# Two of eight row-tile pairs of an up-projection in seven block products

## The chip, the core and the metric

The kernel runs on one core of a Trainium2 chip. The metric is the device time of one execution in microseconds (us). The median of three runs of the kernel before is 1767.04 us (1766.61 to 1767.25).

The engines that matter here are TensorE (PE in the profile; PEld is its weight load), VectorE (DVE), ScalarE (ACT), GpSimd (POOL), which issues some transfers, and SyncE (SP), which issues the weight loads. Each engine takes its instructions strictly in the order in which the built program has them.

## The reference

One decoder layer on 256 tokens of width 2048, all in fp32. An input projection of 16896 columns feeds a gated linear recurrence (16 heads) and a dilated attention (12 heads). Their outputs are projected, gated, added and projected once more (`w_out`) onto the residual. Then comes the part that the change touches, the convolutional feed-forward, and a last RMSNorm:

```
hup = u @ w_up                       # (256, 2048) @ (2048, 11264)
hc  = causal depthwise conv of width 3 over the tokens of hup, + conv_b
a, b = hc[..., :5632], hc[..., 5632:]
h   = h + (gelu(a) * b) @ w_down     # (256, 5632) @ (5632, 2048)
```

## The kernel before

**Three matmuls per product.** An fp32 operand is split into two float32r parts: `hi`, the operand rounded to float32r by a copy on ACT, and `lo`, the rest `raw - hi`, computed on DVE. Each product of an activation block and a weight block is the sum of three float32r matmuls: low activation by `hi` weight, high by `hi`, high by `lo` (lines 386, 387 and 388 of `moving_step`). The activations are the stationary operand (128x128), the weights the moving one (128x512).

**The weight stream.** All weights lie in memory in the order of their use, cut into units of sixteen 128x128 tiles (1 MB each). `stream_spec` writes that order down. `load` fetches a unit into one of three `raw` buffers on SP's queue. `split` makes `hi` and `lo` of it in two halves of 128x1024 (lines 248 and 249), each in a pool of four buffers. `next_tiles` splits two units ahead and loads three ahead of the unit in use.

**The feed-forward.** `w_up` is worked through in 11 blocks of 512 columns of the first half (`ua0` to `ua10`) and 512 of the second (`ub0` to `ub10`). For each, `moving` accumulates 16 row tiles and two token halves into two of four main PSUM banks (`psm`). `up` then scales the banks on ACT, transposes them on PE into side banks (`pss`, four), and runs the convolution on ACT and DVE (lines 800 to 802). After the gate and another split (`ff`), `w_down` follows in two parts (`PARTS`): after six blocks and after the other five, each adding to the residual `h`.

**What sets the order.** Apart from the first stage, the order of each engine's instructions is made by a scheduler at build time from the order of the code, the buffers and the dependencies. It puts instructions of other work between those that would have to wait.

Of the kernel before, what the change touches and what calls it, by code (L numbers as in the profile page):

```python
# [33 lines left out]
PARTS = ((0, 6), (6, NBLK))  # L34
EPS = 1e-6
UNIT = 16
LOOKAHEAD = 2
# [108 lines left out]
def hybrid_block(ctx, tc, x_p, x_t, weights, g1, gf, params, c_rope, c_mask0, c_mask1, c_level, out):  # L148
# [39 lines left out]
    raws, splits = {}, {}  # L188
# [34 lines left out]
    xu = [w4([2, 2, T], f"xu{i}", F32R) for i in range(KD // 2)]  # L223
# [8 lines left out]

    def split(u):
        if u >= NUNITS or u in splits:
            return
        load(u)
        parts = []
        half = UNIT * P // 2
        for s in range(2):
            hi = wp.tile([P, half], F32R, tag="hi", name=f"hi{u}_{s}", bufs=4)  # L240
            lo = wp.tile([P, half], F32R, tag="lo", name=f"lo{u}_{s}", bufs=4)
            n = 2 if u == 0 else 1
            w = half // n
            for q in range(n):
                raw = raws[u][:, s * half + q * w : s * half + (q + 1) * w]
                if u < KD // 2 and q == 0:
                    split_x(2 * u + s)
                last[0] = act.activation(hi[:, q * w : (q + 1) * w], raw, AF.Copy)  # L248
                last[1] = vec.tensor_tensor(lo[:, q * w : (q + 1) * w], raw, hi[:, q * w : (q + 1) * w].bitcast(F32), op=ALU.subtract)  # L249
            parts.append((hi, lo))  # L250
        splits[u] = parts
# [29 lines left out]

    def next_tiles(n):

        i = pos[0]
        u, r = divmod(i, UNIT)
        if r == 0:
            for v in range(u, u + LOOKAHEAD + 1):
                split(v)
            load(u + LOOKAHEAD + 1)
            pump(SIDE_US)  # L290
# [99 lines left out]
    def moving(parts, k0, nk, name):  # L390

        pst = [main_bank(f"{name}_{m}") for m in range(2)]
        for k in range(k0, k0 + nk):
            moving_step(pst, parts, k, k0, nk)
        return pst

# [146 lines left out]
    def hgrn_side(g, f, k, q, gt, v):  # L543
# [22 lines left out]
        for li, b in enumerate(LEVELS):  # L566
            ps = side_bank(f"lv{g}_{b}")
            psv = ps.rearrange("p (m h t) -> p m h t", m=2, h=HG)
            ks = sb.tile([P, M], F32, tag="o2", name=f"ks{g}_{b}", bufs=6)
# [22 lines left out]
            if b < 64:  # L592
                new = sb.tile([P, half], F32, tag=f"tot{b}", name=f"tot{g}_{b}", bufs=1)
# [8 lines left out]
        a01 = sb.tile([P, HG, P], F32, tag="a01", name=f"a01_{g}", bufs=1)  # L602
# [4 lines left out]
        for m in range(2):  # L607
# [6 lines left out]
            sq = sb.tile([P, M], F32, tag="o2", name=f"osq{g}_{m}", bufs=6)  # L614
# [7 lines left out]
            o1 = sb.tile([P, HG, P], F32, tag="o2", name=f"oo{g}_{m}", bufs=6)  # L622
# [70 lines left out]
    drain()  # L693

# [9 lines left out]
    mixed = [[w4([4, 2, P], f"mix{j}_{m}", F32R) for m in range(2)] for j in range(NJ)]  # L704
# [4 lines left out]

    def stage(name):  # L710
        return sb.tile([P, 512], F32, tag="o2", name=name, bufs=6)
# [29 lines left out]
    hv = [w4([2, 2, T], f"hv{i}", F32R) for i in range(KD // 2)]  # L741

    def hv_parts(k, m):
        t = hv[k // 2][:, k % 2]
        return t[:, 0, m * P : (m + 1) * P], t[:, 1, m * P : (m + 1) * P]
# [16 lines left out]
    for j in range(NJ):  # L762
# [4 lines left out]
        for i in range(2):  # L767
            pt = side_bank(f"ht{j}_{i}").rearrange("p (c t) -> p c t", c=2)
            for c in range(2):
                for m in range(2):  # L770
                    n = (2 * i + c) * P
                    pe.transpose(pt[:, c, m * P : (m + 1) * P], h[:, m, n : n + P], ident)
            for c in range(2):
                k = 4 * j + 2 * i + c
                d = hv[k // 2][:, k % 2]
                act.activation(d[:, 0], pt[:, c], AF.Copy, scale=pc("g2", k))
                vec.scalar_tensor_tensor(d[:, 1], pt[:, c], pc("g2", k), d[:, 0].bitcast(F32), op0=ALU.mult, op1=ALU.subtract)
# [3 lines left out]


    def up(b, c0, name):

        pst = moving(hv_parts, 0, KD, name)
        ups = []
        for m in range(2):
            u = stage(f"{name}u{m}")
            act.activation(u, pst[m], AF.Copy, scale=rstd2[:, m : m + 1])
            ups.append(u)  # L790
        t = w4([FB, T], f"{name}c")
# [14 lines left out]
    for part, (b0, b1) in enumerate(PARTS):  # L806
        ff = [w4([2, 2, T], f"ff{part}_{i}", F32R) for i in range((b1 - b0) * FB // 2)]
        for b in range(b0, b1):
            a = up(b, b * FB, f"ua{b}")
# [5 lines left out]
            g = up(b, NFF + b * FB, f"ub{b}")  # L815
# [6 lines left out]
        if part:  # L822
# [72 lines left out]
```

## Time and profile before

| | |
|---|---|
| median of the runs shown | 1767.04 us |
| the profiled execution's own time | 1768.19 us |
| its span, first to last instruction | 1766.4 us |
| mean granted TensorE clock | 0.998 |
| PE busy | 1749.9 us (99% of the span) |
| DVE busy | 1092.5 us (62%) |
| ACT busy | 888.6 us (50%) |
| memory read | 321.41 MB, 183 GB/s over the span |
| instructions | 21297 |

A row of groups gives line, engine, operation, the tile written and those read, shapes and count; then total busy time and the mean of one in ns; then the engine's idle time just ahead of them, with what ended it. A matmul's mean (390 ns) is from its start to its modelled end; since matmuls overlap, the distance from one start to the next is what a matmul costs. A row of the timeline gives start and duration in us; "x2" merges neighbours. The up-projections of the first six blocks run from about 1024 to 1298 us, `w_down`'s first part to 1427 us, the other five blocks to 1655 us, its second part to 1754 us.

### The profile page before, as it was taken

Reading aid. Unit: us, or ns where it says so; the run is one execution under the profiler, and the core shown is the slowest. Engines: PE = TensorE matmul, PEld = TensorE weight load, DVE = VectorE, ACT = ScalarE, POOL = GpSimd, SP = SyncE. Lnnn points to the kernel's source line nnn. Section 1 sums busy time; section 2 is a strip of 40 time slices with the busy share of each in tenths; the row PEclk is TensorE's granted clock in tenths of the full one; section 3 lists DMA queues with packets and bytes.
Section 4 is the critical chain, followed back from the end, with each engine's and each line's share of the span. In section 5 each row is a group of like instructions: output and inputs, shape, how many; then the busy total and the mean of one; then the engine's idle time right before and its main releaser. Section 6 shows DMA issues by size and latency. Waiting matters only on the chain.

```text
span 1766.4 us, 21297 instructions
## 1 busy us (share of the span) xinstructions
PE 1749.9 (99%) x8472; PEld 1463.5 (83%) x8472; DVE 1092.5 (62%) x1295; ACT 888.6 (50%) x1084; POOL 9.4 (1%) x24
## 2 busy tenths in 40 slices
PE   9999999999999999999999999999999999999997
PEld 7888888888888888888888888888888888888885
DVE  7765575777768675445565556666664456666654
ACT  6444465545454555444445455555543345555442
POOL 0000000000000000000000000000000000000000
PEclk9999999999999999999999999999999999999999
DMA  7665634544444444555556555455555554555552
GB/s 274 220 209 201 228 143 145 179 165 179 167 167 167 166 168 167 191 190 191 191 185 227 185 191 185 177 186 191 182 189 196 196 188 176 184 215 185 188 197 98
DMA packets 48371, 328.02 MB, mean 186 GB/s; under 512 B 5600, under 2 KB 5856, under 8 KB 10128
## 3 DMA queue, kind: packets, MB, share of 16 engines
q1 hardware_dynamic: 45648, 318.28, 50.7%
q0 software_dynamic: 1472, 5.24, 1.1%
q10 hardware_dynamic: 1152, 3.15, 0.5%
q8 instruction: 66, 1.08, 0.2%
q14 instruction: 33, 0.27, 0.0%
HBM read 321.41 MB, written 2.10 MB: 183 GB/s over the span
## 4 chain that ended last, share of the span: by engine, by line
PE 97%; DVE 1%; DMA 1%; ACT 0%; issue 0%; SPq 0%; DVEq 0%; ACTq 0%
PE ub L387 5%; PE ub L386 5%; PE ub L388 5%; PE ua L387 5%; PE ua L388 5%; PE ua L386 5%; PE dn L387 5%; PE dn L386 5%; PE dn L388 5%; PE egp L388 3%; PE egp L386 3%; PE egp L387 3%; PE ak L299 3%; PE aq L299 2%; PE wo L388 2%; PE gp L387 2%
## 5 line engine op out<-in xcount | busy, mean ns | idle before, releaser
L249 DVE TENSOR_TENSOR lo<-raw,hi 128x1024 fp32r<-128x1024 f32 (+1 forms) x602 | 734.5, 1221 | 575.5 <-ACT hi L248 565.9
L248 ACT ACTIVATE hi<-raw 128x1024 fp32r<-128x1024 f32 (+1 forms) x602 | 636.0, 1057 | 763.3 <-PE dn L387 127.3
L387 PE MATMUL ub<-hi,hv 128*128 128x512 f32 x352 | 139.2, 395 | 0.0
L387 PE MATMUL ua<-hi,hv 128*128 128x512 f32 x352 | 138.8, 394 | 0.0
L387 PE MATMUL dn<-hi,ff 128*128 128x512 f32 x352 | 137.4, 390 | 0.0
L386 PE MATMUL ub<-hi,hv 128*128 128x512 f32 x352 | 137.3, 390 | 0.0
L386 PE MATMUL ua<-hi,hv 128*128 128x512 f32 x352 | 137.3, 390 | 0.0
L388 PE MATMUL ub<-lo,hv 128*128 128x512 f32 x352 | 137.2, 390 | 0.0
L388 PE MATMUL ua<-lo,hv 128*128 128x512 f32 x352 | 137.2, 390 | 0.0
L386 PE MATMUL dn<-hi,ff 128*128 128x512 f32 x352 | 137.1, 390 | 0.0
L388 PE MATMUL dn<-lo,ff 128*128 128x512 f32 x352 | 137.1, 389 | 0.0
L386 PE MATMUL egp<-hi,xu 128*128 128x512 f32 x256 | 100.7, 393 | 0.0
L388 PE MATMUL egp<-lo,xu 128*128 128x512 f32 x256 | 99.9, 390 | 0.0
L387 PE MATMUL egp<-hi,xu 128*128 128x512 f32 x256 | 99.8, 390 | 0.0
L386 PEld LDWEIGHTS ub<-hi,hv 128*128 128x128 f32 x352 | 66.1, 188 | 14.0
L386 PEld LDWEIGHTS dn<-hi,ff 128*128 128x128 f32 x352 | 66.1, 188 | 13.8
L386 PEld LDWEIGHTS ua<-hi,hv 128*128 128x128 f32 x352 | 66.1, 188 | 13.8
L388 PEld LDWEIGHTS dn<-lo,ff 128*128 128x128 f32 x352 | 66.1, 188 | 13.6
L387 PEld LDWEIGHTS dn<-hi,ff 128*128 128x128 f32 x352 | 66.1, 188 | 13.5
L388 PEld LDWEIGHTS ua<-lo,hv 128*128 128x128 f32 x352 | 66.2, 188 | 13.1
L387 PEld LDWEIGHTS ua<-hi,hv 128*128 128x128 f32 x352 | 66.2, 188 | 13.0
L388 PEld LDWEIGHTS ub<-lo,hv 128*128 128x128 f32 x352 | 66.2, 188 | 13.0
(435 smaller groups left out, 3154.9 us busy)
## 6 DMA issues: line engine op xcount, KB each, us to landing
raw<-weights SPq DMA_DIRECT2D x298, 1024.0 KB, 4.8
h<-x_t ACTq DMA_DIRECT2D x4, 512.0 KB, 7.5
xt<-x_p SPq DMA_DIRECT2D x3, 512.0 KB, 10.3
xs_q<-aqraw POOLq DMA_DIRECT2D x6, 256.0 KB, 6.8
xs_k<-akraw POOLq DMA_DIRECT2D x6, 256.0 KB, 7.2
raw<-weights SPq DMA_DIRECT2D x4, 256.0 KB, 4.8
raw<-weights SPq DMA_DIRECT2D x2, 512.0 KB, 8.1
gfb<-gf POOLq DMA_DIRECT2D x2, 512.0 KB, 6.6
```

The source lines that it names most:

```text
L248: last[0] = act.activation(hi[:, q * w : (q + 1) * w], raw, AF.Copy)
L249: last[1] = vec.tensor_tensor(lo[:, q * w : (q + 1) * w], raw, hi[:, q * w : (q + 1) * w].bitcast(F32), op=ALU.subtract)
L299: pe.matmul(ps, hi, pair, start=(k == 0), stop=False, skip_group_check=True)
L386: pe.matmul(pst[m], xl, hi, start=(k == k0), stop=False)
L387: pe.matmul(pst[m], xh, hi, start=False, stop=False)
L388: pe.matmul(pst[m], xh, lo, start=False, stop=(k == k0 + nk - 1))
```

## The change

The 16 row tiles of a `w_up` block are taken as eight pairs, and a pair's product with the two column halves is a product of two 2x2 block matrices: token halves by row tiles, and row tiles by column blocks. The string `UP_PAIRS = "SPAPSAPA"` gives each pair one of three modes.

- **S** (two pairs): Strassen's method, in the form with seven products and shared sums. `split_s` forms four sums of weight blocks (`q1` to `q4`) on DVE and splits seven blocks into `hi` and `lo` rather than four; 21 matmuls.
- **P** (three pairs): eight products, 24 matmuls, arranged so that they add into the same seven PSUM banks. The activation differences `d1` and `d2` are operands.
- **A** (three pairs): as P, but the `lo` part of the unit's second half is made by ACT writing `-hi` (a copy of raw rounded, scaled by -1) and a transfer from POOL that adds `raw` to it in SBUF.

`sevenfold` accumulates a whole block in seven banks: four main ones and three side ones. `unfold` reads them back: four ACT copies and seven DVE instructions give the four 128x512 results (`c11`, `c21` for the first column half, `c12`, `c22` for the second), which `convolved` transposes as before. `operands` makes the sums of activation blocks once per pair, after the last `w_out` product. `w_down` is done in four parts rather than two, and the SBUF pools are rearranged: some close when their stage ends, and the S splits have a pool of their own. In the first block the pairs are taken in the order 1, 2, 0, 3, 5, 4, 6, 7.

The diff, cut to its core:

```diff
-PARTS = ((0, 6), (6, NBLK))
+PARTS = ((0, 3), (3, 6), (6, 9), (9, NBLK))
+UP_PAIRS = "SPAPSAPA"
+STAGES = 8
...
+    def split_s(u):
+        r = raws[u].rearrange("p (b n) -> p b n", b=4)
...
+        q = pool.tile([P, 2, 512], F32, tag="q", name=f"q{u}", bufs=1)
+        ah, al = pair_tiles(wp, (("hi", 4), ("lo", 4)), "sa")
+        eh, el = pair_tiles(pool, (("se", 4), ("se", 4)), "se")
+        fh, fl = pair_tiles(pool, (("se", 4), ("se", 4)), "sf")
+        g = pool.tile([P, 2, 512], F32R, tag="sg", name=f"sg{u}", bufs=1)
+        vec.tensor_tensor(q[:, 0], r[:, 0], r[:, 3], op=ALU.add)
+        two_parts(ah, al, r[:, 0:2])
+        vec.tensor_tensor(r[:, 3], r[:, 3], r[:, 2], op=ALU.add)
+        vec.tensor_tensor(q[:, 1], q[:, 0], r[:, 2], op=ALU.add)
+        two_parts(eh, el, r[:, 2:4])
+        vec.tensor_tensor(r[:, 0], q[:, 1], r[:, 1], op=ALU.add)
+        two_parts(fh, fl, q[:])
+        two_parts(g[:, 0], g[:, 1], r[:, 0])
...
                 last[0] = act.activation(hi[:, q * w : (q + 1) * w], raw, AF.Copy)
-                last[1] = vec.tensor_tensor(lo[...], raw, hi[...].bitcast(F32), op=ALU.subtract)
+                if s and MODES.get(u) == "A":
+                    act.activation(lo, raw, AF.Copy, scale=-1.0)
+                    nc.gpsimd.dma_start(lo, raw, accum_op=ALU.add)
+                else:
+                    last[1] = vec.tensor_tensor(lo[...], raw, hi[...].bitcast(F32), op=ALU.subtract)
...
+    PRODUCTS = {
+        "S": ((1, "a11", "11"), (7, "x3", "q3"), (6, "x2", "q2"), (2, "a12", "21"), (4, "a22", "q4"), (5, "x1", "q1"), (3, "x4", "22")),
+        "P": (
+            (2, "a11", "11"), (2, "a12", "21"), (4, "a21", "11"), (4, "a22", "21"),
+            (5, "a21", "12"), (5, "a22", "22"), (3, "d1", "12"), (3, "d2", "22"),
+        ),
+    }
+    PRODUCTS["A"] = PRODUCTS["P"]
...
+    def sevenfold(ops, modes_of, order, name):
+        banks = {i: (main_bank if i < 5 else side_bank)(f"{name}_{i}") for i in range(1, 8)}
...
+        for i in order:
+            w = next_pair()
+            for b, x, n in PRODUCTS[modes_of[i]]:
+                (xh, xl), (wh, wl) = ops[i][x], w[n]
...
+                pe.matmul(banks[b], xl, wh, start=b in fresh, stop=False)
+                pe.matmul(banks[b], xh, wh, start=False, stop=False)
+                pe.matmul(banks[b], xh, wl, start=False, stop=left[b] == 0)
...
+    def unfold(p, r, name):
...
+        act.activation(t, p[1], AF.Copy)
+        vec.tensor_tensor(v, p[6], t, op=ALU.subtract)
+        c11, c21, c12, c22 = (stage(f"{name}c{n}") for n in ("11", "21", "12", "22"))
+        act.activation(c11, p[1], AF.Copy, scale=r0)
+        act.activation(c12, v, AF.Copy, scale=r0)
+        act.activation(c21, v, AF.Copy, scale=r1)
+        vec.scalar_tensor_tensor(c21, p[7], r1, c21, op0=ALU.mult, op1=ALU.add)
+        vec.scalar_tensor_tensor(c11, p[2], r0, c11, op0=ALU.mult, op1=ALU.add)
+        vec.scalar_tensor_tensor(c22, p[5], r1, c21, op0=ALU.mult, op1=ALU.add)
+        vec.scalar_tensor_tensor(c12, p[5], r0, c12, op0=ALU.mult, op1=ALU.add)
+        vec.scalar_tensor_tensor(c21, p[4], r1, c21, op0=ALU.mult, op1=ALU.subtract)
+        vec.scalar_tensor_tensor(c12, p[3], r0, c12, op0=ALU.mult, op1=ALU.add)
...
-            a = up(b, b * FB, f"ua{b}")
+            a0, a1, g0, g1_ = unfold(sevenfold(hv, UP_PAIRS, up_order(b), f"up{b}"), rstd2, f"up{b}")
+            a = convolved((a0, a1), b * FB, f"ua{b}")
...
-            g = up(b, NFF + b * FB, f"ub{b}")
+            g = convolved((g0, g1_), NFF + b * FB, f"ub{b}")
```

How the change moves instructions is shown at three places; with the change, all three are where block 1 ends and block 2 begins. In the rows a number after a tile's name is the unit of the weight stream (`lo184`) or the block (`up1c11`); the last number is the buffer's own. Unit 184 is the S pair with which block 2 begins, 185 a P pair, and 181 is the A pair in sixth place of block 1.

First, VectorE where a block's sums are finished. Before (here the first half of block 2, `ua2`), only the splits of the next units and the convolution stand there:

```order
L249 TENSOR_TENSOR lo187_1_8699<-raw187_8668,hi187_1_8698 128x1024
L249 TENSOR_TENSOR lo188_0_8729<-raw188_8702,hi188_0_8728 128x1024
L249 TENSOR_TENSOR lo188_1_8733<-raw188_8702,hi188_1_8732 128x1024
L249 TENSOR_TENSOR lo189_0_8763<-raw189_8736,hi189_0_8762 128x1024
L249 TENSOR_TENSOR lo189_1_8767<-raw189_8736,hi189_1_8766 128x1024
L801 SCALAR_TENSOR_TENSOR ua2c_8800<-ua2t0_8801,par_77,ua2c_8800 128x255
L801 SCALAR_TENSOR_TENSOR ua2c_8800<-ua2t1_8812,par_77,ua2c_8800 128x255
```

With the change, at the boundary between blocks 1 and 2:

```order
L275 TENSOR_TENSOR q184_8647<-raw184_8621 128x512
L311 TENSOR_TENSOR lo183_0_8613<-raw183_8589,hi183_0_8612 128x1024
L277 TENSOR_TENSOR raw184_8621<-raw184_8621 128x512
L278 TENSOR_TENSOR q184_8647<-q184_8647,raw184_8621 128x512
L260 TENSOR_TENSOR sel184_8651<-raw184_8621,seh184_8650 128x1024
L260 TENSOR_TENSOR sal184_8649<-raw184_8621,sah184_8648 128x1024
L260 TENSOR_TENSOR sfl184_8653<-q184_8647,sfh184_8652 128x1024
L280 TENSOR_TENSOR raw184_8621<-q184_8647,raw184_8621 128x512
L311 TENSOR_TENSOR lo185_0_8694<-raw185_8667,hi185_0_8693 128x1024
L260 TENSOR_TENSOR sg184_8654<-raw184_8621,sg184_8654 128x512
L535 SCALAR_TENSOR_TENSOR up1c11_8731<-up1_2_8428,rstd2_r_8027,up1c11_8731 128x512
L311 TENSOR_TENSOR lo185_1_8698<-raw185_8667,hi185_1_8697 128x1024
```

The whole split of unit 184 now stands ahead of `up1c11`; three more `unfold` instructions follow (`up1c22`, `up1c12`, `up1c21`), and then the convolution.

Second, TensorE at such a place. Before, the transposes of a finished half (`ua1t`) stand among the matmuls of the next one (`ub1`):

```order
L388 MATMUL ua1_1_8323<-lo179_1_8363,hv7_7313 128x512
L386 MATMUL ub1_0_8488<-hi180_0_8392,hv0_7306 128x512
L797 MATMUL ua1t0_8465<-ident_79,ua1u0_8460 128x128
L797 MATMUL ua1t1_8476<-ident_79,ua1u0_8460 128x128
L387 MATMUL ub1_0_8488<-hi180_0_8392,hv0_7306 128x512
```

With the change:

```order
L520 MATMUL up1_3_8429<-lo183_1_8617,hvd7_8017 128x512
L936 MATMUL ua1t0_8745<-ident_82,up1c11_8731 128x128
L936 MATMUL ua1t1_8756<-ident_82,up1c11_8731 128x128
L518 MATMUL up2_1_8796<-sah184_8648,hvs0_7469 128x512
L519 MATMUL up2_1_8796<-sah184_8648,hvs0_7469 128x512
L520 MATMUL up2_1_8796<-sal184_8649,hvs0_7469 128x512
L518 MATMUL up2_2_8797<-sah184_8648,hvs0_7469 128x512
L519 MATMUL up2_2_8797<-sah184_8648,hvs0_7469 128x512
L520 MATMUL up2_2_8797<-sal184_8649,hvs0_7469 128x512
L518 MATMUL up2_2_8797<-hi185_0_8693,hva1_7485 128x512
L519 MATMUL up2_2_8797<-hi185_0_8693,hva1_7485 128x512
L936 MATMUL ua1t0_8745<-ident_82,up1c21_8732 128x128
```

The first two transposes stand right behind the block's last matmul, and twelve more stand eight matmuls later, behind `up1c21`.

Third, SP's queue of weight loads, with the semaphores that each load waits for (DMAHW: an earlier load; DMASW: a transfer that POOL issued). Before:

```order
L213 DMA raw180_8366<-weights 128x2048 [waits DMAHW2_49,DVE_49]
L213 DMA raw181_8400<-weights 128x2048 [waits DMAHW3_49,DVE_49]
L213 DMA raw182_8434<-weights 128x2048 [waits DMAHW4_49,DVE_49]
L213 DMA raw183_8498<-weights 128x2048 [waits DMAHW5_49,DVE_49]
L213 DMA raw184_8532<-weights 128x2048 [waits DMAHW6_49,DVE_49]
```

With the change:

```order
L237 DMA raw180_8474<-weights 128x2048 [waits DMAHW2_49,DVE_49]
L237 DMA raw181_8520<-weights 128x2048 [waits DMASW2_49,DMAHW3_49,DVE_49,Activation_49]
L237 DMA raw182_8555<-weights 128x2048 [waits DMAHW4_49,DVE_49]
L237 DMA raw183_8589<-weights 128x2048 [waits DMAHW5_49,DVE_49]
L237 DMA raw184_8621<-weights 128x2048 [waits DMASW3_49,DMAHW6_49,DVE_49,Activation_49]
```

A load into the `raw` buffer of an A pair now waits for that pair's POOL transfer too; unit 184 takes the buffer of unit 181.

More of the change, by code (lines that the diff above doesn't have):

```diff
@@ L56, in mov, with pairs @@
                 spec.append((name, k * P, col + c * P))
+    def pairs(name, n1, n2, k0, modes_of, order):
+        for i in order:
+            mode = modes_of[i]
+            k2, k1 = k0 + 2 * i, k0 + 2 * i + 1
+            modes[len(spec) // UNIT] = mode
+            blocks = [(k1, n1), (k2, n1), (k2, n2), (k1, n2)] if mode == "S" else [(k1, n1), (k2, n1), (k1, n2), (k2, n2)]
+            for k, n in blocks:
+                for c in range(4):
+                    spec.append((name, k * P, n + c * P))
     o_q, o_f, o_i, o_g = 0, 2048, 4096, 6144
@@ L220, in load @@
             nc.sync.dma_start(par, params)
[L223 removed]
+    xu = [sbe.tile([P, 2, 2, T], F32R, tag="xu", name=f"xu{i}", bufs=KD // 2) for i in range(KD // 2)]
     def x_pair(k):
@@ L280, in drain, with begin_unit, next_pair @@
         debt[0] = 0.0
+    def begin_unit(u):
+        for v in range(u, u + LOOKAHEAD + 1):
+            split(v)
+        load(u + LOOKAHEAD + 1)
+        pump(SIDE_US)
+    def next_pair():
+        u = pos[0] // UNIT
+        begin_unit(u)
+        pos[0] += UNIT
+        if MODES[u] == "S":
+            return splits[u]
+        (h0, l0), (h1, l1) = splits[u]
+        return {
+            n: (h[:, i * 512 : (i + 1) * 512], l[:, i * 512 : (i + 1) * 512])
+            for n, h, l, i in (("11", h0, l0, 0), ("21", h0, l0, 1), ("12", h1, l1, 0), ("22", h1, l1, 1))
+        }
     def next_tiles(n):
@@ L286, in next_tiles @@
         if r == 0:
[L287 to L290, printed above, removed]
+            begin_unit(u)
         h, q = divmod(r, UNIT // 2)
@@ new lines, in unfold @@
+    def unfold(p, r, name):
+        r0, r1 = r[:, 0:1], r[:, 1:2]
+        t, v = stage(f"{name}t"), stage(f"{name}v")
+        act.activation(t, p[1], AF.Copy)
[10 more added lines that the diff above has]
+        vec.scalar_tensor_tensor(c12, p[3], r0, c12, op0=ALU.mult, op1=ALU.add)
+        return c11, c21, c12, c22
@@ L740, in hybrid_block @@
         ht.append(t)
[L741 to L745, printed above, removed]
+    hv = []
     def square_sums(name):
@@ L780, in hybrid_block, with convolved @@
     rstd2 = rsqrt_tokens(ss2, "rstd2")
[L783 to L791, printed above, removed]
+    mid.close()
+    late["pool"] = late["stage"] = ctx.enter_context(tc.tile_pool(name="sbl", bufs=1))
+    def convolved(ups, c0, name):
+        t = late["pool"].tile([P, FB, T], F32, tag="uc", name=f"{name}c", bufs=2)
         for i in range(2):
```

94 lines of the change are left out of this document (70 added, 24 removed).

## The prediction

> **What bounds the kernel now.** I read the page's busy times and its chain first, then the stretches, the timeline of one block, the groups by shape, and the transfers. Busy times and chain:
>
> ```profile
> PE 1749.9 (99%) x8472; PEld 1463.5 (83%) x8472; DVE 1092.5 (62%) x1295; ACT 888.6 (50%) x1084; POOL 9.4 (1%) x24
> ...
> PE 97%; DVE 1%; DMA 1%; ACT 0%; issue 0%; SPq 0%; DVEq 0%; ACTq 0%
> ```
>
> TensorE is the bound in every stage. The stretches (length, then busy time of PE, PEld, DVE, ACT, POOL with instruction counts, clock, transfer share, GB/s) show where it is not:
>
> ```profile
> 1024.00:1297.60 273.60, 273.60 (x1250) 224.99 (x1249) 170.02 (x210) 152.73 (x187) 0.00 (x0) 1.00 0.52 185
> 1297.60:1427.50 129.90, 129.90 (x574) 107.61 (x573) 64.71 (x58) 50.93 (x48) 0.00 (x0) 1.00 0.54 193
> ...
> 1753.80:1766.40 12.60, 0.61 (x3) 0.18 (x1) 6.06 (x16) 3.05 (x7) 0.00 (x0) 0.68 0.45 166
> ```
>
> In the first six up-projection blocks PE has no gap, while DVE is busy 170.02/6 = 28.3 us a block and ACT 25.5. Only the tail of 12.6 us is without PE, and the change leaves it. So every matmul taken away counts in full, as long as nothing makes PE wait. The price of a matmul is the distance between starts: between these two rows of the timeline stand 33 steps (the 32 rows between are alike), and 7.48/33 = 0.2267 us.
>
> ```profile
> 1092.12 0.39 PE L386 MATMUL ub<-hi,hv 128*128 128x512 f32 x1
> ...
> 1099.60 0.39 PE L386 MATMUL ub<-hi,hv 128*128 128x512 f32 x1
> ```
>
> A block's length is read from the chain, from one block's transposes to the next:
>
> ```profile
> 1081.27 0.32 PE ua1t L797 x2
> 1082.98 0.66 PE ua1t L797 x6
> ...
> 1126.83 0.32 PE ua2t L797 x2
> ```
>
> 45.56 us, of which 192 matmuls are 43.5 and 16 transposes 1.96.
>
> **What is removed.** An S pair needs 21 matmuls in place of 24, so 6 fewer a block and 66 over 11 blocks: 66 x 0.2267 = **15.0 us**. Transposes and `w_down`'s matmuls keep their number. A block then takes PE 186 x 0.2267 + 1.96 = 44.1 us.
>
> **What is added to DVE and ACT.** The prices, by shape:
>
> ```profile
> L249 DVE TENSOR_TENSOR lo<-raw,hi 128x1024 fp32r<-128x1024 f32 x598 | 731.8, 1225 | 574.9 <-ACT hi L248 565.5 <-PE lv L577 5.3 <-PE lv L601 1.5
> L683 DVE SCALAR_TENSOR_TENSOR g<-gp,rst,g 128x512 f32<-128x512 f32 x8 | 6.0, 745 | 0.0
> L628 DVE TENSOR_TENSOR oo<-oo,g 128x512 f32<-128x512 f32 x8 | 5.5, 692 | 0.3
> L248 ACT ACTIVATE hi<-raw 128x1024 fp32r<-128x1024 f32 x598 | 633.5, 1060 | 762.8 <-PE dn L387 127.3 <-PE ua L387 93.1 <-PE ub L387 86.7
> L403 ACT ACTIVATE v<-vp,rst 128x512 f32<-128x512 f32 x8 | 5.5, 684 | 4.7 <-PE vp L388 4.7
> L552 ACT ACTIVATE pr<-qp 128x512 fp32r<-128x512 f32 x8 | 4.8, 616 | 0.0
> ```
>
> An S split costs DVE three `lo` of 1.225, one of 512 columns (0.69) and four sums (0.69 each): 7.1 us for 2.45 before, so +9.4 a block. An A pair saves it one `lo`: -3.7 a block. `unfold` adds seven of 0.745: +5.2. DVE comes to 39.2 of 44.1 us (89%). ACT gets 1.7 more per S pair, 1.06 more per A pair, and four copies for the four scalings it had: 25.5 + 3.4 + 3.2 = 32.1 us (73%). Neither exceeds PE, so by busy time alone nothing is lost; what decides is order.
>
> **The wait that I expect.** Today a weight load waits for the last `lo` of the buffer's former unit and lands 4.8 us later. These are the waits of SP's queue (total, times, longest), and the landing of `raw` (least, median, most):
>
> ```profile
> SPq L213 <- DVE lo L249: 1343.0, 253, 8.1
> ...
> DMA to landing us min/median/max: 4.0/4.8/10.7
> ```
>
> With the change, unit 184 (the S pair that opens block 2) takes the buffer of unit 181 (an A pair), so its load also waits for that pair's POOL transfer; call its time from issue to landing T. On DVE, `up1c11` and `up1c21` are queued behind the whole split of 184, and PE's transposes behind them. Count from the end of block 0's last product:
>
> - PE: 2 transposes, 7 matmuls, 14 transposes = 3.55 us, then 179 matmuls; block 1's products end at 44.1. `up1c21` is wanted 2 transposes and 8 matmuls later, at 46.2.
> - Unit 179's second `hi` needs a buffer that PE frees 50 matmuls after 3.55, at 14.9; with 0.2 for the matmul's end, ACT has it done at 16.2. DVE then does `lo179_1`, `sal180`, two `ff`, `sel180` and a sum (1.225 + 1.225 + 2 x 0.69 + 1.225 + 0.69), less 0.06 for each that overlaps its neighbour: 21.6. ACT follows with `sg180` (0.62), `hi181_1` and the negated copy (1.06 each): 24.2. There the POOL transfer can start.
> - `raw184` lands at 24.2 + T + 4.8. DVE needs from there to `up1c21` five sums or halves of 0.69, six `lo` of 1.225 and four reads of PSUM at 0.745 = 13.8, less 14 overlaps (0.8), plus 0.4 where `sel184` waits for ACT: 13.4. So `up1c21` is done at 42.4 + T, and PE waits **T - 3.8**.
>
> The overlap of 0.06 is the end of the first of these rows (943.71) against the start of the second:
>
> ```profile
> 942.48 1.23 DVE L249 TENSOR_TENSOR lo<-raw,hi 128x1024 fp32r<-128x1024 f32 x1 [1.49 <-ACT hi L248]
> 943.65 1.37 DVE L766 TENSOR_TENSOR h<-h,wo 128x512 f32<-128x512 f32 x2
> ```
>
> This holds where an up block follows one that itself followed one (1 to 2, 4 to 5, 7 to 8). Behind the first block of a part (3 to 4, 6 to 7, 9 to 10) no convolution is in the way: the buffer frees after 81 matmuls (18.4), the copy ends at 20.7, `c21` at 38.9 + T, wanted at 42.2 + 2.1 = 44.3: PE waits **T - 5.4**. From block 0 to 1 the S unit's buffer comes from another S unit, and four blocks are followed by `w_down`: no such wait there.
>
> **What T is.** The trace has no accumulating transfer. Nearest are transfers that POOL issued: `gfb`, 512 KB each in this very stage, and `xs_q`, 256 KB each from SBUF to SBUF. Landing (least, median, most) of `gfb`, its two issues, and landing of `xs_q`; then the weight queue:
>
> ```profile
> DMA to landing us min/median/max: 4.8/6.6/8.4
> ...
> 1563.84 0.54 POOL L825 DMA_DIRECT2D gfb<-gf x1 [1367.98 <-ACT hi L248]
> 1566.53 0.54 POOL L825 DMA_DIRECT2D gfb<-gf x1 [2.14 <-issue]
> ...
> DMA to landing us min/median/max: 4.9/6.8/7.4
> ...
> q1 hardware_dynamic: 45648, 318.28, 50.7%
> ```
>
> The two `gfb` follow each other by 2.7 us, and the `xs` come in pairs too; an A transfer has POOL's queue to itself, so I take the least, 4.8, which hardly depends on size. Adding needs a second read: at the weight queue's pace (0.507 x 1766.4/318.28 = 2.81 us per MB) half a MB is 1.5 us in series and 0 if overlapped; I take 0.7. **T = 5.5**; the ends are 4.8 and 8.4 + 1.5 = 9.9, and below 4.8 only if an SBUF source lands faster than any row. Three boundaries lose 1.7 and three 0.1: **5.4 us**.
>
> [...]
>
> PE's own waits for the `lo` that the transfer makes have more room: in sixth place it is wanted 121 matmuls after 3.55, at 31.0, so T may be 6.8; in eighth place the copy ends at 35.4 and it is wanted at 41.8, T 6.4. At 5.5 they cost nothing; beyond that up to 5 blocks lose twice the excess.
>
> **The start of block 0.** PE is at the S pair's second product 8 transposes and 53 matmuls after the last `w_out` matmul, 13.0 us. ACT has ten copies of 256 to 1024 columns, two square sums and a table load queued ahead of that product's `hi`, about 12 us in all from the rows above and these:
>
> ```profile
> 1015.39 0.83 ACT L776 ACTIVATE hv<-ht,par 128x256 fp32r<-128x256 f32 x2
> 1016.25 1.28 ACT L321 ACT_TABLE_LOAD   x1
> ```
>
> Its `lo` on DVE ends near 14.5: **1.5 us** of wait once, 0 to 3.
>
> **At nothing.** Sixteen more additions to `h` (11 us) fall into `w_down`, where DVE is idle half the time; without that cover they would cost those 11 us. 33 more transfers of 512 KB share engines that are busy 52%. Up to the last `w_out` matmul PE's order is unchanged.
>
> **Sum.** 15.0 - 5.4 - 1.5 = 8.1 us saved: 1768.19 - 8.1 = 1760.1 by the profiled execution's own time, which is 1.15 above the median; against the median, **1759 us**.
>
> **Rivals.**
>
> 1. *The transfer lands in time.* T below 3.8: only the start costs, 1767.0 - 13.5 = 1753.5. Against it: no POOL row is under 4.8. [...] Chance 0.17.
> 2. *It lands later than 7.0 and the kernel is slower.* At T = 7.3 (`gfb`'s median and 0.7): three boundaries lose 3.5, three 1.9, the start 1.5, and five blocks 0.9 and 0.5 at their A pairs: 24.7, so 1777. From T = 7.0 this outweighs the saving by 0.2%. For it: both medians; against: those came in pairs. Chance 0.24.
> 3. *DVE's in-order queue becomes the bound.* At 89% its gaps decide: ACT and DVE hand each other every split, and if handovers leave DVE idle 15% of the time, a block is 39.2/0.85 = 46.1, 0.6 more than today, 1767 + 11 x 0.6 + 1.5 = 1775. It is slower from 14%. For it: DVE's idle time today is all behind ACT's `hi`; against: that idle time has slack, since ACT in turn waits for PE's buffers. Chance 0.09.
> 4. *Gain and loss cancel.* T between 6.3 and 7.0: within 3.5 us of before. Chance 0.14.
>
> My forecast (T from 3.8 to 6.3) has 0.36. That the S pairs save no matmuls is ruled out by the built order, which has 66 fewer.
>
> **How the numbers follow.** 0.2% is about what a measurement can tell from no change. Faster: 0.36 + 0.17 = 0.53; the same 0.14; slower 0.24 + 0.09 = 0.33. The range reaches from the full saving, 1753, to T about 7.6 at 1781; beyond are T up to 9.9.
>
> **What would show it.** In the changed kernel, an up block of 44.1 us between `w_down`-side boundaries and some 45.9 where block 2, 5 or 8 opens; PE idle ahead of `ua1t` and its like, released by DVE's `c11` or `c21`; the first sum of the S split released by `raw`; landings of the POOL transfers near 5.5; PE matmuls down by 66. Landings above 7, or PE waiting for `lo` behind a transfer, would make rival 2 right; no PE gap at the boundaries, rival 1; DVE above 95% in the up blocks with gaps behind ACT, rival 3.

## The result: 1.06% slower

| | before | with the change |
|---|---|---|
| median | 1766.82 us (1765.48 to 1767.25, 4 runs) | 1785.72 us (1783.8 to 1786.25, 4 runs) |
| ratio | | 1.0106, 95% interval 1.0089 to 1.0124 |
| the profiled execution's own time | 1768.19 us | 1786.24 us |
| matmuls | 8472 | 8406 |

The forecast was 1759 us, with a range from 1753 to 1781. The 66 matmuls are gone, and the kernel is 18.9 us slower.

From the page of the changed kernel, its busy times and the shares of its chain of waits:

```profile
PE 1754.5 (98%) x8406; PEld 1453.0 (81%) x8406; DVE 1204.1 (67%) x1499; ACT 951.7 (53%) x1177; POOL 38.3 (2%) x57
...
PE 89%; DVE 4%; DMA 4%; issue 2%; ACT 1%; SPq 0%; DVEq 0%; POOLq 0%; ACTq 0%
```

PE is busy 4.6 us longer than before, with 66 matmuls fewer, and 11% of the chain lies elsewhere, where it was 3%. So two things happened: matmuls take longer, and PE waits. (In the kernel before, the up-projections begin at 1012.51 us, with the first row of the stage shown below, and the first `w_down` product follows at 1285.93; the stretch from 1024 to 1298 us given further up is cut some 12 us late.)

**Longer matmuls.** The timelines of PE in one stage with the same instructions in the same order (`egp`, a projection far ahead of the change), of the kernel before and of the changed one; between the two rows of each stand 12 steps from start to start:

```profile
718.28 0.39 PE L388 MATMUL egp<-lo,xu 128*128 128x512 f32 x1
...
721.00 0.39 PE L388 MATMUL egp<-lo,xu 128*128 128x512 f32 x1
```

```profile
718.38 0.40 PE L465 MATMUL egp<-hi,xu 128*128 128x512 f32 x1
...
721.18 0.40 PE L465 MATMUL egp<-hi,xu 128*128 128x512 f32 x1
```

2.72/12 = 0.2267 us before, 2.80/12 = 0.2333 now: 6.7 ns more for each matmul, at a granted clock of 1.00 in both (718 to 721.2 us). The groups by shape agree, and show the other sign where `xu` is the moving operand. Before, then changed:

```profile
L387 PE MATMUL egp<-hi,xu 128*128 128x512 f32 x256 | 99.8, 390 | 0.0
L299 PE MATMUL ak<-xu,hi 128*128 128x512 f32 x192 | 68.1, 399 | 0.2 <-ACT av L403 0.2
```

```profile
L465 PE MATMUL egp<-hi,xu 128*128 128x512 f32 x256 | 101.2, 396 | 0.0
L377 PE MATMUL ak<-xu,hi 128*128 128x512 f32 x192 | 66.7, 390 | 0.0
```

The slow matmuls are those with `xu`, `mix` or the differences `d1` and `d2` as the stationary operand, or as the moving one a weight block that the S split keeps in its own pool, most of them sums: all that now stands in one of the new pools. (Their means in the up blocks are 394 to 396 ns with the differences, `hvd`, where the products with `hva` have 390 to 393.) The first `w_up` product comes 7.9 us later, though all before it is the same work. Before, and changed:

```profile
1012.51 0.39 PE L386 MATMUL ua<-hi,hv 128*128 128x512 f32 x1
```

```profile
1020.43 0.39 PE L518 MATMUL up<-hi,hva 128*128 128x512 f32 x1
```

In each up block 66 matmuls are of this kind (36 with `d1` or `d2`, 30 with such a weight block), 0.44 us a block, 4.9 us in all.

**PE's gaps.** A gap here is what a distance between the starts of two successive matmuls has above the usual step, where it is over 0.33 us. From the first `w_up` product on, the kernel before has none. The changed kernel has 38, together 20.0 us:

| where | us | in blocks |
|---|---|---|
| ahead of the convolution's transposes | 5.7 | 0, 1, 3, 4, 6, 7, 9 |
| ahead of `seh` of the S pair that opens a block | 3.7 | 4, 7, 10 |
| at a `lo` made by a POOL transfer | 4.3 | 0, 2, 3, 5, 8 |
| in the last part of `w_down`: waiting for a weight's `lo` (1.3) and for block 10's `ff` (3.0), then at half the pace (1.6) | 5.9 | |
| elsewhere | 0.4 | |

The sum is -15.0 + 7.9 + 4.9 + 20.0 = +17.8 us, and the profiled executions differ by 1786.24 - 1768.19 = 18.05.

The waits behind these gaps, by engine (total, times, longest):

```profile
SPq L237 <- DMA lo<-raw: 320.4, 33, 13.3
...
DVE q L275 <- DMA raw<-weights: 40.8, 10, 5.5
...
PEld up L520 <- DMA lo<-raw: 5.7, 8, 1.4
...
PEld dn L464 <- DVE ff L960: 4.2, 4, 3.3
```

SP's weight queue waits for each of the 33 POOL transfers, and DVE stands 41 us at the first sum of an S split waiting for weights. DVE and PE at the boundary from block 1 to block 2, with the last product of block 0 for the count below:

```profile
1094.54 0.75 DVE L534 SCALAR_TENSOR_TENSOR up1c<-up,rstd_r,up1c 128x512 f32<-128x512 f32 x1
1100.76 0.69 DVE L275 TENSOR_TENSOR q<-raw 128x512 f32<-128x512 f32 x1 [5.46 <-DMA raw<-weights]
...
1110.07 0.74 DVE L535 SCALAR_TENSOR_TENSOR up1c<-up,rstd_r,up1c 128x512 f32<-128x512 f32 x1
...
1113.18 0.74 DVE L538 SCALAR_TENSOR_TENSOR up1c<-up,rstd_r,up1c 128x512 f32<-128x512 f32 x1
```

```profile
1064.59 0.40 PE L520 MATMUL up<-lo,hvd 128*128 128x512 f32 x1
...
1112.74 0.39 PE L519 MATMUL up<-hi,hva 128*128 128x512 f32 x1
1113.97 0.87 PE L936 MATMUL ua1t<-ident,up1c 128*128 128x128 f32 x6 [0.84 <-DVE up1c L538]
```

This is the wait of the prediction: DVE idle until `raw184` lands at 1100.7, then the whole split, in the order of the built program, then `up1c21` at 1113.9, and PE there 1.0 us earlier.

The gap ahead of `seh` is another wait. ACT, DVE and PE at the beginning of block 4:

```profile
1270.65 2.01 ACT L306 ACTIVATE hi<-raw 128x1024 fp32r<-128x1024 f32 x2 [4.28 <-DMA raw<-weights]
...
1275.31 1.02 ACT L939 ACTIVATE ua3c<-ua3t,par 128x256 f32<-128x256 f32 x2
```

```profile
1276.77 0.86 DVE L941 SCALAR_TENSOR_TENSOR ua3c<-ua3t,par,ua3c 128x254 f32<-128x254 f32 x2
```

```profile
1272.59 0.40 PE L518 MATMUL up<-seh,hvx 128*128 128x512 f32 x1
...
1277.38 0.48 PE L518 MATMUL up<-seh,hvx 128*128 128x512 f32 x1 [1.16 <-ACT hi L306]
```

PE does not wait for the S split here: the same `seh` served a product 4.8 us earlier, and ACT had finished it 18.6 us before the gap ended. The `hi` that the row names is no operand of this product. In all three of these gaps PE goes on 0.1 us after DVE has ended the first of the two instructions that one row of L941 merges, a read of the transposes' bank `ua3t` (or `ua6t`, `ua9t`). A block needs three of the four side banks, and the transposes of the block before hold all four until the convolution has read them; so PE most likely waits for a bank. The convolution begins late: ACT has two `hi` ahead of it, and the first of them waited 4.28 us for weights.

And the end, where PE has come to the last block's `ff` too early:

```profile
1734.71 0.39 PE L466 MATMUL dn<-lo,ff 128*128 128x512 f32 x1
1737.97 0.80 PE L464 MATMUL dn<-hi,ff 128*128 128x512 f32 x1 [2.87 <-DVE ff L960]
1738.56 0.63 PE L465 MATMUL dn<-hi,ff 128*128 128x512 f32 x1
1738.99 0.63 PE L466 MATMUL dn<-lo,ff 128*128 128x512 f32 x1
```

After the gap of 3 us the next matmuls start 0.43 us apart rather than 0.227, until 1741.1.

### The profile page after: what moved, and what is told of

It is laid out like the page before. It is cut to its first block, busy times and chain, and to the rows that moved or that the text cites. A ratio compares the mean times of both kernels' runs of the same rounds, so it can differ in the third digit from the quotient of the medians.

```text
span 1784.5 us, 21599 instructions
## 1 busy us (share of the span) xinstructions
PE 1754.5 (98%) x8406; PEld 1453.0 (81%) x8406; DVE 1204.1 (67%) x1499; ACT 951.7 (53%) x1177; POOL 38.3 (2%) x57
## 4 chain that ended last, share of the span: by engine, by line
PE 89%; DVE 4%; DMA 4%; issue 2%; ACT 1%; SPq 0%; DVEq 0%; POOLq 0%; ACTq 0%
PE up L520 7%; PE up L519 7%; PE up L518 7%; PE dn L464 4%; PE dn L465 4%; PE dn L466 4%; PE egp L464 3%; PE egp L466 3%; PE egp L465 3%; DMA lo<-raw 3%; PE ak L377 2%; PE gp L464 2%; PE gp L466 2%; PE vp L464 2%; PE vp L466 2%
## 5 line engine op out<-in xcount | busy, mean ns | idle before, releaser
L306 ACT ACTIVATE hi<-raw 128x1024 fp32r<-128x1024 f32 (+1 forms) x558 | 588.0, 1056 | 703.1 <-PE dn L465 108.0
L311 DVE TENSOR_TENSOR lo<-raw,hi 128x1024 fp32r<-128x1024 f32 (+1 forms) x525 | 638.8, 1219 | 434.8 <-ACT hi L306 426.4
L520 PE MATMUL up<-lo,hva 128*128 128x512 f32 x396 | 155.5, 393 | 2.7 <-DMA lo<-raw 2.7
L518 PE MATMUL up<-hi,hva 128*128 128x512 f32 x396 | 154.7, 391 | 0.0
L519 PE MATMUL up<-hi,hva 128*128 128x512 f32 x396 | 154.6, 390 | 0.0
L520 PEld LDWEIGHTS up<-lo,hva 128*128 128x128 f32 x396 | 74.3, 188 | 21.4 <-DMA lo<-raw 5.7
L519 PEld LDWEIGHTS up<-hi,hva 128*128 128x128 f32 x396 | 74.3, 188 | 16.0
L518 PEld LDWEIGHTS up<-hi,hva 128*128 128x128 f32 x396 | 74.4, 188 | 15.9
L377 PE MATMUL ak<-xu,hi 128*128 128x512 f32 x192 | 66.7, 390 | 0.0
L309 POOL DMA_DIRECT2D lo<-raw x33 | 28.8, 872 | 1491.0 <-ACT lo L308 1360.4
L466 PEld LDWEIGHTS egp<-lo,xu 128*128 128x128 f32 x256 | 48.1, 188 | 11.6
L465 PEld LDWEIGHTS egp<-hi,xu 128*128 128x128 f32 x256 | 48.1, 188 | 11.2
L464 PEld LDWEIGHTS egp<-hi,xu 128*128 128x128 f32 x256 | 48.1, 188 | 11.1
## 6 DMA issues: line engine op xcount, KB each, us to landing
xt<-x_p SPq DMA_DIRECT2D x3, 512.0 KB, 10.4
```

Source lines behind the costliest of these rows:

```text
L309: nc.gpsimd.dma_start(lo, raw, accum_op=ALU.add)
L377: pe.matmul(ps, hi, pair, start=(k == 0), stop=False, skip_group_check=True)
L464: pe.matmul(pst[m], xl, hi, start=(k == k0), stop=False)
L465: pe.matmul(pst[m], xh, hi, start=False, stop=False)
L466: pe.matmul(pst[m], xh, lo, start=False, stop=(k == k0 + nk - 1))
L518: pe.matmul(banks[b], xl, wh, start=b in fresh, stop=False)
```

## The experiments

### Where the operands stand

The built programs say at which byte of a partition each tile begins. In the kernel before, weights (`hi`, `lo`) and activations (`w4`) all begin at 3008 modulo 4096. In the changed kernel the new pools follow the activations' pool, at whose end the small tiles take 544 bytes; so `xu`, `mix`, the differences and the sums begin at 3552 modulo 4096, 544 bytes off the weights. Two experiments moved the pools without any change in the order of instructions.

**e1: the kernel before, with 32 bytes ahead of its activations.**

```diff
+    small([8], "pad", "pad", 1)
     xt = [w4([4, T], f"xt{q}") for q in range(4)]
```

> The kernel before, in which one unused tile of 32 bytes stands ahead of the pool of activations: every activation operand then begins 32 bytes past a multiple of 64 in its partition, while raw, hi and lo stay on multiples of 64; the order of instructions is the same. Placement theory (the profile of the change shows 233 to 235 ns from start to start where the stationary operand lies in a pool that begins 32 bytes past a multiple of 64, and 227 where it lies on one): 5856 matmuls with an activation as the stationary operand go from 227 to 233.7 ns, +39 us, and the 832 pairs of matmuls with xu as the moving one go from 353 to 347 ns, -5.5 us: 1767 + 33.5 = about 1800 us. Rival (the longer step comes from other traffic in the changed kernel, not from the addresses): 1767 us.

Measured: 1797.7 us, ratio 1.0179 (1.0162 to 1.0196). One unused tile of 32 bytes costs the old kernel 31 us, near the 33.5 worked out from the pace in the changed kernel. Its group, where the kernel before has a mean of 390:

```profile
L388 PE MATMUL egp<-hi,xu 128*128 128x512 f32 x256 | 101.2, 395 | 0.0
```

The longer step thus needs nothing of the change's other traffic: none of it is in this kernel.

**e2: the changed kernel, with its new pools on multiples of 64 bytes.**

```diff
-            ss = small([HG], f"oss{g}_{m}", "oss")
+            ss = small([HG], f"oss{g}_{m}", "oss", 3)
```

> The changed kernel with 32 bytes more in the pool of small tiles (three buffers for oss in place of two), so that all pools behind it begin on a multiple of 64; the order of instructions is the same. Placement theory: the 7.3 us lost before the first w_up product come back, and in each up block 66 matmuls (36 with d1 or d2 stationary, 30 with a Strassen sum moving) lose 6.7 ns each, 0.44 us a block, 4.9 us in all: 1785.7 - 12.2 = 1773.5 us, up to 1777 if PE then waits longer for DVE. Rival (contention): 1785.7 us.

Measured: 1790.73 us, ratio 1.0139 (1.0123 to 1.0154). The expectation failed, and with it the rule in it: `xu` now begins on a multiple of 64, and 576 bytes off the weights, and is as slow as stationary operand as before, while its gain as moving operand is lost.

```profile
L465 PE MATMUL egp<-hi,xu 128*128 128x512 f32 x256 | 101.0, 394 | 0.0
...
L377 PE MATMUL ak<-xu,hi 128*128 128x512 f32 x192 | 68.0, 396 | 0.0
```

So it is not the multiple that counts. The next theory was the distance between the two operands.

**e5: the changed kernel, with the small tiles among the constants,** ahead of all other pools. Weights and activations are then 0 bytes apart modulo 4096, and neither is on a multiple of 64.

```diff
     def small(shape, name, tag, bufs=2):
-        return sb.tile([P] + list(shape), F32, tag=tag, name=name, bufs=bufs)
+        return const.tile([P] + list(shape), F32, tag=tag, name=name, bufs=bufs)
```

> The changed kernel with its small tiles (544 bytes) moved from the pool of activations to the constants, which stand ahead of all other pools. Weights and activations then stand in the same place relative to each other, modulo 4096 bytes, as in the kernel before, but all of them 32 bytes past a multiple of 64; the order of instructions is the same. Theory (what counts is where the stationary and the moving operand stand relative to each other, not on what multiple either begins): 227 ns from start to start with xu, mix or d1 and d2 stationary, as in the kernel before, and 353 ns for a pair of matmuls with xu moving: 7.3 us less up to the first w_up product and 4.9 us less in the up blocks, 1785.7 - 12.2 = 1773.5 us, up to 1777 where PE then waits for DVE. Rival (an operand that does not begin on a multiple of 64 costs 6.7 ns, and a second one too): 240 ns, 1800 us or more.

Measured: 1775.22 us (1771.32 to 1777.44), ratio 1.0053 (1.0036 to 1.007): 10.5 us less than the change, where 12.2 was expected. The first `w_up` product starts at 1009.66 us, 10.8 us earlier than in the change; that this is also 2.9 us earlier than in the kernel before was not followed up.

```profile
L465 PE MATMUL egp<-hi,xu 128*128 128x512 f32 x256 | 99.7, 389 | 0.0
```

**e11 and e12: e1 with 128 and with 256 bytes.**

> e1_before_shift32 with 128 bytes in place of 32. If operands must stand in the same place modulo 512 bytes (the length of one row of a 128-column operand, by which operands within a tile differ): about 1798 us, as with 32. If modulo 128 is enough: 1767 us.

> The same with 256 bytes. If operands must stand in the same place modulo 512 bytes: about 1798 us. If modulo 256 is enough: 1767 us.

Measured: 1796.78 us with 128 bytes, ratio 1.0172 (1.0158 to 1.0186); 1766.84 us with 256, ratio 1.0002 (0.9992 to 1.0011). The same group in the one and in the other:

```profile
L388 PE MATMUL egp<-hi,xu 128*128 128x512 f32 x256 | 101.1, 395 | 0.0
```

```profile
L388 PE MATMUL egp<-hi,xu 128*128 128x512 f32 x256 | 99.7, 389 | 0.0
```

So 128 bytes are not enough, and 512 not needed: the distances tried agree with a rule modulo 256. Distances of 32 (e1, and the change: 544 is 32 modulo 256) and 64 (e2: 576) cost 6.7 ns a matmul, 128 a little less (over all such matmuls the mean step is 232.5 ns in e11, 233.3 in e1 and 227.1 in the kernel before); 0 and 256 cost nothing.

### The waits in the up blocks

**e4: no S pair opens a block.**

```diff
 def up_order(b):
-    return (1, 2, 0, 3, 5, 4, 6, 7) if b == 0 else tuple(range(KD // 2))
+    return (1, 2, 0, 3, 5, 4, 6, 7)
```

> The changed kernel with the order of pairs of its block 0 (P, A, S, P, A, S, P, A) in every block, so that no S pair opens a block and unfold's c11 and c21 stand ahead of the S split in DVE's queue. Theory of the prediction (c11 and c21 are queued behind the split of the S pair that opens the next block, whose weights land late): PE's gaps ahead of the convolution's transposes (5.6 us in seven of the eleven blocks) and those ahead of seh in blocks 4, 7 and 10 (3.7 us) go, 1785.7 - 9.3 = about 1776.5 us. Rival (DVE has too little slack in a block wherever the S pair stands, and the wait appears at another place): within 3 us of 1785.7.

Measured: 1798.33 us, ratio 1.0182 (1.0167 to 1.0197), slower still: its gaps come to 32.7 us. With an A pair in eighth place, an S pair in third place takes its weight buffer from an A pair again, and the weights stay late:

```profile
DVE q L275 <- DMA raw<-weights: 29.3, 14, 4.7
```

Moving the S pair does not remove the cause. Splits run two units ahead, so the split of a third pair falls where the block begins, and its first sum still stands ahead of `c21` on DVE. That sum waits for its weights where block 1 ends, and PE's gap ahead of the transposes there is 4.2 us (3.2 in block 0, by the same wait):

```profile
1114.96 0.69 DVE L275 TENSOR_TENSOR q<-raw 128x512 f32<-128x512 f32 x1 [4.67 <-DMA raw<-weights]
```

Three transfers of 10.7 to 11.0 us, in blocks 4, 7 and 10, add gaps of 2.0 to 2.3 us each at their `lo`, and after five of the pauses 36 matmuls in all run at half the pace, about 7 of the 32.7 us.

**e6: the sixth pair in mode P**, so that no POOL transfer stands ahead of the S pair's weights.

```diff
-UP_PAIRS = "SPAPSAPA"
+UP_PAIRS = "SPAPSPPA"
```

> The changed kernel with mode P in place of A for the sixth pair (SPAPSPPA), so that the buffer of the S pair that opens the next block is freed by DVE and not by POOL's adding transfer; DVE gets one lo of 1.23 us more a block. Theory of the prediction (that transfer makes the weights of the S pair late, and c11 and c21 are queued behind its split): PE's gaps ahead of the convolution's transposes (5.6 us in all) and ahead of seh in blocks 4, 7 and 10 (3.7 us) go: 1785.7 - 9.3 = about 1776.5 us. Rival (DVE has no slack in a block, whoever frees the buffer): 1784 us or more.

Measured: 1778.03 us, ratio 1.0062 (1.0047 to 1.0077), 7.7 us less than the change. The gaps ahead of the transposes are all gone, as expected. Those ahead of `seh` stay, in six blocks rather than three (4.8 us for 3.7): in all six PE goes on 0.1 us after DVE's read of the transposes' bank, and in four of them no `hi` ends just before. Instead the gaps at the `lo` of the transfers fall from 4.3 us to 0.1, which the expectation did not count. DVE's wait at the first sum:

```profile
DVE q L275 <- DMA raw<-weights: 11.9, 7, 3.4
```

**e7: no transfers at all** (`"SPPPSPPP"`).

> The changed kernel with mode P in place of A throughout (SPPPSPPP): no adding transfers; DVE does three more lo a block, by busy time 42.9 of 44.1 us. Theory of the prediction (the transfers cause PE's waits in the up blocks, DVE's load alone costs nothing): the gaps ahead of the transposes (5.6 us), ahead of seh (3.7) and ahead of the lo of the transfers (3.5) go: 1785.7 - 12.8 = about 1773 us. Rival (DVE's queue is the bound): slower than 1786, and at 97% busy 1795 or more.

Measured: 1772.02 us, ratio 1.0033 (1.0022 to 1.0043), 13.7 us less. Up to the last block's `ff` no gap is over 0.12 us. The stretch from 1024 to 1110 us (length, then busy PE, PEld, DVE, ACT, POOL) and the first transposes of two successive blocks:

```profile
1024.00:1110.00 86.00, 86.00 (x384) 69.86 (x383) 77.74 (x104) 57.16 (x74) 0.00 (x0) 1.00 0.52 190
```

```profile
1109.48 0.38 PE L936 MATMUL ua1t<-ident,up1c 128*128 128x128 f32 x2
...
1154.02 0.38 PE L936 MATMUL ua2t<-ident,up2c 128*128 128x128 f32 x2
```

DVE is busy 90% of it, more than in the change, and PE never waits. A block takes 44.54 us: the 44.1 of the prediction and the 0.44 of the 66 slow matmuls. Of the gaps 6.4 us are left, 5.7 of them at the end. DVE's load was not the bound; the transfers, and the weights that they delay, were what made PE wait in the up blocks.

**e8: e5, with a weight buffer of its own for the S pairs** (and six stage buffers for eight, to make room).

```diff
-STAGES = 8
+STAGES = 6
...
-        r = wp.tile([P, UNIT * P], F32, tag="raw", name=f"raw{u}", bufs=3)
+        if MODES.get(u) == "S" and "pool" in late:
+            r = late["pool"].tile([P, UNIT * P], F32, tag="raws", name=f"raw{u}", bufs=1)
+        else:
+            r = wp.tile([P, UNIT * P], F32, tag="raw", name=f"raw{u}", bufs=3)
```

> e5_after_relative with a weight buffer of its own for the S pairs (and six buffers for stages in place of eight, to make room), so that the weights of an S pair no longer wait for the split or the transfer of the pair three places earlier, and the other six pairs share three buffers. Theory (late weights of the S pairs make DVE late where a block ends): the gaps ahead of the transposes (5.6 us) and of seh (3.7) go: 9 us less than e5, about 1764.5 us. Rival (DVE's busy time and order make it late, not the landing): within 3 us of e5.

Measured: 1758.78 us, ratio 0.9955 (0.994 to 0.997): 16.4 us less than e5, where 9 was expected, and faster than the kernel before. All 33 transfers are still there; the S pairs' weights no longer wait for them.

```profile
DVE q L278 <- DMA raw<-weights: 8.2, 7, 2.0
```

```profile
1099.80 0.38 PE L939 MATMUL ua1t<-ident,up1c 128*128 128x128 f32 x2
...
1143.82 0.38 PE L939 MATMUL ua2t<-ident,up2c 128*128 128x128 f32 x2
```

44.02 us a block, where the prediction has 44.1. The profiled executions of e5 and e8 differ by 11.9 us (1771.32 and 1759.45), and so do their gaps, 21.3 and 9.4 us; e5's median lies 3.9 us above its profiled execution, which makes up most of the rest. The gaps ahead of the transposes and of `seh` fall from 10.4 to 1.0 us. Those at a `lo` fall too, from 5.8 to 0.6: in sixth place of blocks 2, 5 and 8 the transfers take 7.1, 6.5 and 6.4 us rather than the 9.0, 8.9 and 9.3 of e5. Of the 9.4 us left 7.3 are at the end.

### The end

**e3: the changed kernel, with the first two column blocks of the last `w_down` part interleaved.**

```diff
+        for js in down_groups(b1):     # ((0, 1), (2,), (3,)) in the last part, else one by one
+            psts = {j: [main_bank(f"dn{part}_{j}_{m}") for m in range(2)] for j in js}
+            for b in range(b0, b1):
+                for j in js:
+                    for k in range(b * FB, (b + 1) * FB):
+                        moving_step(psts[j], ff_parts, k, b0 * FB, (b1 - b0) * FB)
```

> The changed kernel with another order in the last part of w_down alone: the first four row tiles of the first two column blocks, then the last four of both, so that 48 matmuls (10.9 us) rather than 24 (5.4 us) stand between the last w_up product and the first use of block 10's ff. Theory (PE waits at the end because the last part is two blocks long and the last block's convolution, gate and split are late): the gaps there, 1.2 + 3.0 + 0.4 us and six matmuls at half the clock (1.2 us), go: 1785.7 - 6 = about 1780 us. Rival (DVE's and ACT's queues are late by more than 11 us there, so the gap only moves): 1783 us or more.

Measured: 1788.51 us, ratio 1.0125 (1.011 to 1.014): no gain. The order of the changed kernel shows why: the scheduler had already put the second column block's first 24 products ahead of the wait, so 48 stood there without this edit. They are not enough; what was two gaps is now one, and more matmuls at half the pace follow.

```profile
1733.54 0.39 PE L472 MATMUL dn<-lo,ff 128*128 128x512 f32 x1
1738.13 0.80 PE L470 MATMUL dn<-hi,ff 128*128 128x512 f32 x1 [4.21 <-DVE ff L966]
1738.72 0.63 PE L471 MATMUL dn<-hi,ff 128*128 128x512 f32 x1
```

**e9 and e10: e8, with the part of two blocks elsewhere.**

```diff
-PARTS = ((0, 3), (3, 6), (6, 9), (9, NBLK))
+PARTS = ((0, 3), (3, 6), (6, 8), (8, NBLK))     # e9
+PARTS = ((0, 2), (2, 5), (5, 8), (8, NBLK))     # e10
```

> e8_raw_for_s with the parts of w_down at 3, 3, 2 and 3 blocks rather than 3, 3, 3 and 2. Theory (at the end only one finished block of ff stands ahead of the late one, 48 matmuls or 10.9 us against some 15 us from the last w_up product to the last ff): with two finished blocks, 96 matmuls or 21.8 us, the gaps at the end (1.1 + 3.1 + 0.4 us and 13 matmuls at half the clock, 2.6 us) go; the part of two blocks is now in the middle, where no table load stands in ACT's queue (1.3 us less), and loses 2 to 4 us there: e8's 1758.8 - 7.2 + 3 = about 1754.5 us. Rival (wherever two blocks stand, the same is lost): 1758 us or more.

> As e9, but with parts of 2, 3, 3 and 3 blocks. The same theory gives about 1754.5 us, the rival 1758 us or more.

Measured: e9 1756.83 us, ratio 0.9945 (0.9932 to 0.9957), the lowest median of all; e10 1757.41 us, ratio 0.9947 (0.9934 to 0.9961). The numbers lie between theory and rival: with three blocks the end loses 0.8 us rather than 7.3, but the part of two, now in the middle, loses 4.0 in e9.

```profile
1509.89 0.39 PE L523 MATMUL up<-sfl,hvx 128*128 128x512 f32 x1
1512.45 0.78 PE L467 MATMUL dn<-hi,ff 128*128 128x512 f32 x1 [2.17 <-DVE ff L963]
1513.03 0.63 PE L468 MATMUL dn<-hi,ff 128*128 128x512 f32 x1
```

Where the part of two stands in the middle, without the table load, it still loses more than half of what it lost at the end: more than half of the loss is its length. The gain of e9 over e8, 2 us, is at the edge of what these runs can tell.

## Why the prediction was wrong, point by point

- **"Up to the last w_out matmul PE's order is unchanged", costed at nothing.** This step failed first. The order is unchanged, and the time is not: 7.9 us up to the first `w_up` product. The same premise stands in "the price of a matmul is the distance between starts", 0.2267 us for every matmul of its shape: in the up blocks 66 of 186 cost 0.2333, 4.9 us more. Together 12.8 us, by where the rearranged pools put the operands (e1, e5, e11, e12). Without them the change would have been inside the range, and still slower than before (e5: 1775). The forecast had 8.1 us saved and the profiled executions give about 17.8 us lost: of the 25.9 us between them 12.8 are this step, and 13.1 are gaps (20.0 where 6.9 was forecast).
- **What is removed, 15.0 us and a block of 44.1.** Right: 44.02 us where neither wait nor placement is in the way (e8).
- **The wait at 1 to 2, 4 to 5 and 7 to 8.** The mechanism was right and its times nearly exact. From the end of block 0's last product (1064.8): transfer issued 24.4 us later (worked out: 24.2), weights landed at 35.9 (35.5 with the T measured there), `c21` done at 49.1 (48.9). T in this place was 6.5 rather than 5.5, from the transfer's row alone:

```profile
DMA to landing us min/median/max: 6.5/6.5/6.5
```

  PE's gap was nevertheless only 1.0 and not T - 3.8 = 2.7, because PE came there 1.9 us later than worked out, held up by slow matmuls and the boundary before.
- **"At 3 to 4, 6 to 7, 9 to 10: T - 5.4", 0.1 us, and "from block 0 to 1 no such wait".** Undersized: 0.4 to 0.5 ahead of the transposes and 1.2 to 1.3 ahead of `seh`. The second is a wait that the prediction did not count: not for the S split but, most likely, until the late convolution has read a bank that the transposes hold. At 0 to 1 there are 1.3; 1.0 of them stays in e8, whose S pairs have a weight buffer of their own, and its cause is open. All of these gaps together, 9.4 us, stand where 5.4 was forecast. In e6, without the transfer in sixth place, they shrink to 4.8.
- **The A pairs' `lo`, "at 5.5 they cost nothing".** True of the median, 5.3. But T depends on the place: in sixth place of blocks 2, 5 and 8, the last of a part, the chain of waits shows

```profile
1135.19 8.63 DMA lo<-raw
...
1338.66 8.77 DMA lo<-raw
...
1541.54 9.16 DMA lo<-raw
```

  beyond the room of 6.8 that the prediction gave it. The gaps there are about 3 of the 4.3 us. The page's row for all 33, landing in the last column, and the view of their tile, least, median and most:

```profile
lo<-raw POOLq DMA_DIRECT2D x33, 512.0 KB, 5.3
```

```profile
DMA to landing us min/median/max: 4.5/5.3/9.3
```

  The least of them, 4.5 us, is less than the 4.8 of a plain `gfb` of the same size: no run shows the 0.7 us that the prediction, by an estimate, added to T for a second read.
- **The start of block 0, 1.5 us.** Not seen: of the 0.6 us of gaps in the block's products 0.5 are at the `lo` of a transfer, and 0.1 is at an S pair.
- **`w_down` in four parts.** The prediction costed its additions and not its length: "four blocks are followed by w_down: no such wait there". The last part has two blocks, so PE meets the last `ff` after too few matmuls; with the weight's `lo` and the half pace that is 5.9 us, a term that was missing (0.8 where the last part has three blocks, e9).
- **The rivals.** Rival 2 (late transfers, slower) had the places nearly right, at T of 6.5 to 9 where it counts, but its sign only by luck. The gaps of the up blocks, 13.7 us without those of the end, are less than the 15.0 saved, so late transfers alone would have left the kernel about where it was, as in rival 4. What made it slower are the operands' places and the end. Rival 3 (DVE's queue the bound) falls with e7: more work on DVE, no gaps.

## What to carry to other kernels

Before tiles are moved between pools, note where the stationary and the moving operands of the matmuls stand: here 32 bytes of padding cost 31 us, and of the distances tried only 0 and 256 bytes were free. In these runs a slow transfer that freed a buffer was paid for by whatever was loaded into that buffer next and by everything queued behind it; a buffer of its own for that load (e8: 1.6 us of gaps ahead of the transposes, ahead of `seh` and at a `lo`, where e5 has 16.2) took away about as much waiting in the up blocks as leaving out the transfers (e7: 0.7 us of gaps up to the end, where the change has 14.1), without giving their work back to DVE, and changing the order (e4: 32.7 us of gaps in all, where the change has 20.0) took away none. Leaving out the transfers and placing the operands better, both at once, was not tried. And when a stage is cut into more parts, the shortest part must still hold enough work to cover the tail of what feeds it (7.3 us of gaps at the end with a last part of two blocks in e8, 0.8 with one of three in e9).

## What the hardware showed beyond what was expected

- With `xu` stationary the pace of the matmuls changed with the distance of their two operands in a partition: 227 ns at 0 and 256 bytes, 232 to 233 at 32, 64 (576) and 128; these distances agree with a rule modulo 256, and others were not tried. What inside the chip does this was not shown. For matmuls with `xu` moving and weights stationary the pace also varies (means of 390 to 399 ns in these runs), the other way at 32 bytes (390 in e1, 399 in the kernel before), and no rule for it was found.
- After pauses of 2.2 to 4.6 us from one start to the next (after the change, in e3, e4 and e6 to e10), PE ran 6 to 13 matmuls at half the pace, 0.43 us; the granted clock in the profile reads 0.50 there, from 1737.84 to 1741.25 us after the change. Pauses of 3.2 us in e2, 3.3 in e5 and 3.4 in e4 left the pace as it was, and the pause of 2.6 us in e9 was followed by half the pace, so the length of the pause alone does not decide; what does was not shown.
- An adding transfer of 512 KB within SBUF takes 4.5 to 9.3 us from issue to landing after the change (up to 11.0 in e4), by its place in a part of blocks more than by chance: 6.5, 6.5 and 6.7 us in one place, 8.6, 8.8 and 9.2 in another. In e8, where the weight loads stand otherwise, the second place takes 7.1, 6.5 and 6.4; what lengthens it was not isolated.
